# First stage of a streaming-encoder block: another order of column sums, transposes, modulation and masks, and another estimate of transfers in the planner

## The chip, the cores and the metric

The kernel runs on one core of one Trainium2 chip. The metric is the device time of one execution in microseconds (us). Engines are TensorE (PE; its weight loads are listed apart as PEld), VectorE (DVE), ScalarE (ACT), GpSimd (POOL) and SyncE (SP), whose queue starts nearly all transfers. TensorE's clock is shown as the share of full speed that was granted.

## The reference, cut to what matters

One layer of a post-norm encoder block on x of 256 rows by 1024, with a conditioning vector c:

```python
mod = silu(c) @ w_ada + b_ada            # six rows of 1024: sh1, sc1, g1, sh2, sc2, g2
u   = LN(x) * (1 + sc1) + sh1
x   = LN_1(alpha * x + (1 + g1) * Mixer(u))
u   = LN(x) * (1 + sc2) + sh2
x   = LN_2(alpha * x + (1 + g2) * MoE(u))
```

The mixer projects u by one matrix `w_in` of 1024 by 6680. Its first 1536 columns are q, k and v of eight attention heads; the others feed gated linear attention and the gates. The MoE sends each row to 4 of 32 experts. All data are float32.

## The kernel before

**Stages.** The first stage makes q, k and v (columns 0 to 1535 of `w_in`), together with the modulation that u needs. Then come the other projections, attention and the gated linear attention, the branch projections, the output projection, the router, and at last the 32 experts one after the other, whose weights (12 MB each) stream through a ring of buffers. The schedule is written out by hand: each engine executes its instructions in the order in which the program issues them, and waits where one isn't ready.

**The first stage.** The contraction over 1024 is cut into eight steps of 128. For step k two loads are queued on SP, in the order a0, w0, a1, w1 and so on: `first["a", k]` holds 256 columns of `w_ada` (128 of sh1 and 128 of sc1, for all 1024 rows, 1.05 MB in two transfers, rows of 128 elements), `first["w", k]` holds 128 rows of `w_in` by 1536 columns (0.79 MB, rows of 512 elements). `done(...)` hands a buffer back to the ring, which queues the next load. Small loads (`small_loads`) are queued behind step 0.

In each step:

- `ada_sum(k)`: sixteen products of TensorE (listed so; eight in the program) that sum silu(c) times `w_ada` into a bank of PSUM, in four strips of partitions.
- `ada_cols(k, ...)`: VectorE copies the sums to SBUF (`mod`, 128 by 256), TensorE multiplies the copy by a column of `stack` (four listed products), which adds the strips and turns the row into columns; VectorE adds the bias into `shc` (scale and shift as two columns), ScalarE makes `uh` (u rounded to the short float32 format of the matrix products) from the transposed normalized x (`nT`), VectorE makes u in full and `ul = u - uh`.
- `row_parts(k)`: ScalarE rounds the `w_in` rows to `wh`; the rest `wl = w - wh` is made by VectorE (first 512 columns) and GpSimd (second 512 columns), and for v by GpSimd alone. For k = 0 GpSimd makes both halves.
- `three(...)`: each product of u and w is done in three, `wh uh`, `wh ul`, `wl uh`. For q and k these are 24 products of 128x256 in a step, accumulated in four banks (`pqk`), for v six of 128x512 (`pv`).
- two calls of `next(ms)`: the next pieces of the generator `masks`, which builds constants on VectorE that later stages use. Its first piece has thirteen operations, the others three or none.

Ahead of the steps, x (two blocks of 128 rows, `xn[0]`, `xn[1]`) is normalized, block 0 by ScalarE and block 1 by VectorE, and `x_T(hf, tb)` turns half `hf` of block `tb` (four transposes by TensorE, copied out of PSUM by ScalarE for block 0 and by VectorE for block 1).

The order before is: normalize both blocks; transposes of half 0; column sum 0; `row_parts(0)`; modulation 0; transposes of half 1; then for each k: column sum k+1, all 24 products of q and k, `row_parts(k+1)`, modulation k+1, the products of v, two mask pieces.

**The planner.** Behind the first stage, the main products are laced with side tasks (attention scores, gates, row sums). When a side task's next part is issued is decided while the program is built, by `Pace`, a clock per engine and one for the transfers (`at["DMA"]`), advanced by estimated costs. `Pace.dma` estimates a load's end; `lag` is the time from one engine's result to another's use, 1.0 where the earlier access is a transfer.

Of the kernel before, what the change touches and what calls it, by code (L numbers as in the profile page):

```python
# [11 lines left out]
F32R = mybir.dt.float32r  # L12
BF16 = mybir.dt.bfloat16
I32 = mybir.dt.int32
AF = mybir.ActivationFunctionType
OP = mybir.AluOpType
# [4 lines left out]
KC = D // 128  # L21
# [17 lines left out]
FLAT = "p a b -> p (a b)"  # L39
# [40 lines left out]
class Pace:  # L80
# [108 lines left out]
    def dma(self, out, src, size):  # L189
        start = self.at.get("DMA", 0.0)  # L190
        ks = self.blocks(out) if out.space != bass.MemoryType.DRAM else []
        for k in ks:
            w, t = self.last.get(k, ("DMA", 0.0))
            start = max(start, t + self.lag(w, "DMA"))
        end = self.at["DMA"] = start + size / (270000.0 if src.ap[-1][1] <= 128 else 350000.0 if src.ap[-1][1] <= 512 else 400000.0)
        self.note("DMA", [], ks, end)


# [179 lines left out]
def block_kernel(ctx, tc, x, c, w_ada, b_ada, w_in, fox_f_bias, w_gla_gate, b_gla_gate, gla_norm_g,  # L378
# [4 lines left out]
    PE, DVE, ACT, POOL, SP = [Eng(e, n, pace) for e, n in (  # L383
        (nc.tensor, "PE"), (nc.vector, "DVE"), (nc.scalar, "ACT"), (nc.gpsimd, "POOL"), (nc.sync, "SP"))]
# [43 lines left out]
    ring = Ring(new, both, mate, SP)  # L428
# [5 lines left out]
    mm, aux = Bufs(*bank[0:4]), Bufs(*bank[4:8])  # L434
# [4 lines left out]
    gle = Bufs(*cut("GL", 1024))  # L439
# [22 lines left out]
    xn = []  # L462
# [5 lines left out]
    first = {}  # L468
# [139 lines left out]
    def mean_var(st):  # L608
        mv = per.tile([128, 4], F32, tag="mv", bufs=6, name="mv")
        DVE.bn_aggr(mv[:, 0:2], st.rearrange(FLAT))  # L610
        return mv

    def rstd(mv):
        ACT.activation(mv[:, 3:4], mv[:, 1:2], AF.Ln, bias=eps_t)
        ACT.activation(mv[:, 2:3], mv[:, 3:4], AF.Exp, scale=-0.5)

    nT = gst.now([128, 4, T]), gst.now([128, 4, T])
    for tb in range(2):
        st = bn_tile()
        for i in range(2):  # L620
            DVE.bn_stats(st[:, i, :], xn[tb][:, i * 512:(i + 1) * 512])
        mv = mean_var(st)
        rstd(mv)
        if tb:
            DVE.tensor_scalar(xn[tb], xn[tb], mv[:, 0:1], mv[:, 2:3], op0=OP.subtract, op1=OP.mult)
        else:
            DVE.scalar_tensor_tensor(mv[:, 3:4], mv[:, 0:1], -1.0, mv[:, 2:3], op0=OP.mult, op1=OP.mult)
            ACT.activation(xn[tb], xn[tb], AF.Identity, bias=mv[:, 3:4], scale=mv[:, 2:3])


    strict = small("strict", [128, 128], BF16)
# [8 lines left out]
    def masks():  # L640
        trio = consts.now([128, 128])
        DVE.tensor_scalar(trio, jp, 0.0, None, op0=OP.is_ge)
        DVE.tensor_scalar(strict, jp, 0.0, None, op0=OP.is_gt)
        DVE.tensor_scalar(after, jp, 0.0, NEG, op0=OP.is_gt, op1=OP.mult)
        DVE.tensor_copy(identb, ident)
        DVE.memset(onesb, 1.0)
        DVE.tensor_copy(trior[:, 0:128], trio)
        DVE.tensor_copy(trior[:, 128:256], ones)
        xr = consts.now([128, 128], I32)
        DVE.tensor_tensor(xr, pi, ji, op=OP.bitwise_xor)  # L650
        xrf = consts.now([128, 128])
        DVE.tensor_copy(xrf, xr)
        DVE.tensor_scalar(tri64, xrf, 64.0, 1.0 / 16.0, op0=OP.is_lt, op1=OP.mult)
        DVE.tensor_tensor(tri64, tri64, trio, op=OP.mult)
        upm = consts.now([128, 128])
        DVE.scalar_tensor_tensor(upm, jp, 0.0, xrf, op0=OP.is_gt, op1=OP.mult)
        a = consts.now([128, 64])
        yield
        for L in LEVELS:
            yield  # L660
            m = lvl[L] = small(f"lv{L}", [128, 64])
            u3 = upm.rearrange("p (n two l) -> p n two l", two=2, l=L)[:, :, 1, :]
            DVE.tensor_scalar(m.rearrange("p (n l) -> p n l", l=L), u3, float(L), None, op0=OP.is_ge)
            DVE.tensor_scalar(a.rearrange("p (n l) -> p n l", l=L), u3, float(2 * L), None, op0=OP.is_lt)
            DVE.tensor_tensor(m, m, a, op=OP.mult)
# [8 lines left out]
    def split(src, *engines):  # L674

        t, n = pair.now(), src.free_size()
        wh, wl = t[:, 0:n].bitcast(F32R), t[:, 1024:1024 + n].bitcast(F32R)
        ACT.activation(wh, src, AF.Copy)
        if not engines:
            either(wl, src, wh, OP.subtract, WLBIAS)  # L680
        for i, e in enumerate(engines):
            c = slice(i * 512, (i + 1) * 512)
            e.tensor_tensor(wl[:, c], src[:, c], wh[:, c], op=OP.subtract)
        return wh, wl, t
# [60 lines left out]
    def done(i):  # L745
        ring.done(i)
        if last_first in ring.got:
            ring.recall(*early, "YB1")

    def x_T(hf, tb):  # L750
        p = aux.now()
        for q in range(4):
            k = hf * 4 + q
            PE.transpose(p[:, q * 128:(q + 1) * 128], xn[tb][:, k * 128:(k + 1) * 128], ident)
        d, s = nT[hf][:, :, tb * 128:(tb + 1) * 128], p.rearrange("p (a b) -> p a b", a=4)
        if tb:
            DVE.tensor_copy(d, s)
        else:
            ACT.activation(d, s, AF.Copy)
        aux.put(p)  # L760

    def ada_sum(c):

        w = ring[first["a", c]].rearrange("p k a n -> p k (a n)")
        s = pa[:, c % 2 * 256:c % 2 * 256 + 256]
        for k in range(KC):
            j = k % 4
            PE.matmul(s[32 * j:32 * j + 32, :], csrep[:, k, :], w[:, k, :],
                      start=(k < 4), stop=(k >= 4), skip_group_check=True)
        done(first["a", c])  # L770
        return s

    def ada_cols(c, s):
        mod = la.now([128, 256])
        DVE.tensor_copy(mod, s)
        for i in range(2):
            PE.matmul(pb[:, 2 * c + i:2 * c + i + 1], mod[:, i * 128:(i + 1) * 128], stack[:, 0:1], start=True, stop=True)
        la.put(mod)
        DVE.tensor_tensor(shc[:, :, c], pb[:, 2 * c:2 * c + 2], cols[:, 16 + c:32:8], op=OP.add)
        u = nT[c // 4][:, c % 4, :]  # L780
        ACT.activation(uh[:, c, :], u, AF.Identity, bias=shc[:, 0, c:c + 1], scale=shc[:, 1, c:c + 1])
        DVE.tensor_scalar(u, u, shc[:, 1, c:c + 1], shc[:, 0, c:c + 1], op0=OP.mult, op1=OP.add)
        DVE.tensor_tensor(ul[:, c, :], u, uh[:, c, :], op=OP.subtract)

    def row_parts(k):
        w = ring[first["w", k]]
        qk = split(w[:, 0:2, :].rearrange(FLAT), DVE if k else POOL, POOL)
        v = split(w[:, 2, :], POOL)
        done(first["w", k])
        return qk, v  # L790
# [3 lines left out]
            if reg[n] in pair.free:  # L794
                pair.free.remove(reg[n])

    LA = 2
    ms = masks()
    for tb in range(2):
        x_T(0, tb)  # L800
    pa, pb = aux.now(), aux.now()
    sums = {0: ada_sum(0)}
    ahead = {0: row_parts(0)}
    ada_cols(0, sums.pop(0))
    for tb in range(2):
        x_T(1, tb)
    gle.put(*xn)
    pqk, pv = [mm.now() for _ in range(4)], [aux.now(), aux.now()]
    for k in range(KC):
        qk, v = ahead.pop(k)  # L810
        if k + 1 < KC:
            sums[k + 1] = ada_sum(k + 1)
        for cb in range(8):
            cs = slice(cb * 128, (cb + 1) * 128)
            three(pqk[cb // 2][:, (cb % 2) * T:(cb % 2 + 1) * T], (qk[0][:, cs], qk[1][:, cs]), u_of(k),
                  k == 0 and cb % 2 == 0, k == KC - 1)
        pair.put(qk[2])
        if k + 1 < KC:
            ahead[k + 1] = row_parts(k + 1)
            ada_cols(k + 1, sums.pop(k + 1))  # L820
        if k == KC - 1:
            back()
            for q in range(LA):
                prep(q)
            pf = ff_mm()
            fb.put(hold["wfg"])
        for tb in range(2):
            t = slice(tb * 128, (tb + 1) * 128)
            three(pv[tb], (uh[:, k, t], ul[:, k, t]), v[:2], k == 0, k == KC - 1)
        pair.put(v[2])  # L830
        if k == KC - 2:
            aux.put(pa, pb)
        next(ms, None)
        next(ms, None)
        if k == 0:
            small_loads()
        if k == 6:
            for _ in ms:
                pass
            wfg = hold["wfg"]  # L840
            own("YA")
            both("YA")
            pair.free.append(reg["W2"])
            wfh, wfl = hold["wf"] = [shaped(t, [128, KC, 32], F32R) for t in cut("YA", 256, 0, 2)]
            ACT.activation(wfh, wfg, AF.Copy)
            DVE.tensor_tensor(wfl, wfg, wfh, op=OP.subtract)
# [1280 lines left out]
```

## Time and profile before

| | us |
|---|---|
| median of 3 runs | 1266.03 |
| lowest and highest run | 1264.9, 1266.1 |
| profiled execution | 1263.44 |
| its span, first to last instruction | 1261.7 |

| engine | busy us | share of span | instructions |
|---|---|---|---|
| PE | 1167.8 | 93% | 6482 |
| DVE | 492.5 | 39% | 1070 |
| ACT | 266.4 | 21% | 526 |
| POOL | 71.2 | 6% | 52 |

The mean granted clock of TensorE was 0.991, and 471.57 MB were moved, 374 GB/s over the span. Times in the profile count from the start of the span. Names are those of buffers: regions that share memory have joined names (`LQFA`, `YB1NB`), `U1U` holds `uh` and `ul`, `W` and `ADAM` hold `wh` and `wl`, `GL` holds x, `GSGX` holds `nT`, `YAW` the constants of the masks. Nearly every instruction is issued through one helper, so all show its line, L209. Matmuls are pipelined and their ends are modelled: starts are the surer reading. Spans on POOL are rough.

### The profile page before, as it was taken

The page shows a single profiled execution, that of the slowest core. Times are in us where ns is not written, and L with a number is a line of the kernel's source. Part 1 is how long each engine was busy: PE and PEld are TensorE (multiplying, and loading weights), DVE is VectorE, ACT ScalarE, POOL GpSimd, SP SyncE. Part 2 cuts the span into 40 slices and gives each one's busy share as a digit, 9 for nine tenths or more (in the row PEclk, how much of TensorE's full clock was granted, in tenths as well). Part 3 has the DMA queues.
Part 4 walks back from the last instruction along what each step waited for, and adds up shares of the span by engine and source line. Part 5 has one row for each costly group of instructions (what it writes and reads, how often), then busy time and mean ns, then how long its engine had stood idle before and what let it go on. Part 6 is the DMA issues. An engine that isn't in the chain of part 4 may idle for free. (4 is left out here: it accounts for less than half of the span.)

```text
span 1261.7 us, 15755 instructions
## 1 busy us (share of the span) xinstructions
PE 1167.8 (93%) x6482; PEld 598.8 (47%) x6482; DVE 492.5 (39%) x1070; ACT 266.4 (21%) x526; POOL 71.2 (6%) x52
## 2 busy tenths in 40 slices
PE   6999999999899999999998989898989898898995
PEld 4887778898443434344342424343433333342432
DVE  5546654487443323333223222223333232223233
ACT  4345445444411101011010101010111101010101
POOL 3412322010000000000000000000000000000000
PEclk9999999999899999999999999999999999999998
DMA  9953347995999999999999999999999999999994
GB/s 306 314 185 115 135 166 278 397 352 211 394 428 426 429 426 429 426 429 425 430 426 428 427 428 428 428 428 427 428 427 429 427 427 429 426 430 426 430 408 144
DMA packets 74118, 471.57 MB, mean 374 GB/s; under 512 B 8637, under 2 KB 29149, under 8 KB 47034
## 3 DMA queue, kind: packets, MB, share of 16 engines
q1 hardware_dynamic: 73850, 470.23, 91.3%
q8 instruction: 53, 0.87, 0.3%
q10 hardware_dynamic: 192, 0.27, 0.1%
q14 instruction: 23, 0.19, 0.0%
HBM read 469.44 MB, written 1.05 MB: 373 GB/s over the span
## 5 line engine op out<-in xcount | busy, mean ns | idle before, releaser
L209 PE MATMUL b<-U1U,W 128*128 128x256 f32 (+1 forms) x840 | 143.0, 410 | 11.3 <-DMA U1U<-in_w_down_dram 8.4
L209 DVE COPY W<-b 128x512 f32<-128x512 f32 x32 | 22.1, 692 | 295.3 <-PE b L209 295.3
L209 PEld LDWEIGHTS b<-U1U,W 128*128 128x128 f32 (+1 forms) x840 | 86.7, 169 | 69.7 <-issue 61.3
L209 DVE TENSOR_TENSOR W<-b,SP 128x512 f32<-128x512 f32 (+1 forms) x33 | 22.3, 676 | 218.4 <-PE b L209 218.4
L209 DVE TENSOR_TENSOR GL<-b,GL 128x512 f32<-128x512 f32 x124 | 77.0, 683 | 54.0 <-PE b L209 54.0
L209 PE MATMUL b<-YB1NB,W 128*64 128x512 f32 (+2 forms) x440 | 89.4, 528 | 4.5 <-DVE SP L209 3.9
L209 PE MATMUL b<-R2YB,W 128*64 128x512 f32 x344 | 78.3, 595 | 9.8 <-DMA R2YB<-in_w_down_dram 7.9
L209 PE MATMUL b<-YAW,W 128*64 128x512 f32 (+1 forms) x384 | 82.2, 554 | 4.0 <-DVE SP L209 4.0
L209 PE MATMUL b<-GSGX,W 128*64 128x512 f32 x336 | 76.2, 595 | 10.1 <-DMA GSGX<-in_w_down_dram 8.2
L209 PE MATMUL b<-R0R,W 128*64 128x512 f32 (+1 forms) x368 | 80.2, 578 | 5.3 <-DMA R0R<-in_w_up_dram 4.9
L209 PE MATMUL b<-GVKB,W 128*64 128x512 f32 x336 | 78.1, 608 | 6.1 <-DMA GVKB<-in_w_up_dram 6.1
L209 ACT ACTIVATE W<-b 128x512 f32<-128x512 f32 x32 | 19.1, 598 | 302.0 <-PE b L209 302.0
L209 PE MATMUL b<-LQFA,W 128*64 128x512 f32 x336 | 78.1, 607 | 5.0 <-DMA LQFA<-in_w_up_dram 5.0
L209 PE MATMUL b<-ADAM,W 128*64 128x512 f32 x336 | 75.9, 593 | 4.3 <-DVE SP L209 2.7
L209 ACT ACTIVATE SP<-b 128x256 f32<-128x256 f32 (+1 forms) x34 | 12.8, 377 | 306.1 <-PE b L209 306.1
L209 PEld LDWEIGHTS b<-W,QA 128*128 128x128 f32 x512 | 63.1, 200 | 14.1 <-DVE GL L209 11.4
L209 PE MATMUL b<-W,QA 128*128 128x128 f32 x512 | 66.4, 289 | 1.4 <-DVE W L209 1.4
L209 PE MATMUL b<-W,SP 64*128 64x512 f32 (+1 forms) x264 | 63.9, 602 | 0.5 <-DVE W L209 0.5
L209 PEld LDWEIGHTS b<-YB1NB,W 128*64 128x64 f32 (+1 forms) x440 | 35.7, 146 | 55.1 <-issue 45.2
L209 ACT ACTIVATE W<-b,scol 128x128 f32<-128x128 f32 x124 | 47.0, 457 | 65.7 <-PE b L209 59.9
L209 POOL TENSOR_TENSOR GL<-GL,QB 128x512 f32<-128x512 f32 x2 | 2.9, 1426 | 981.5 <-ACT GL L209 981.4
L209 PEld LDWEIGHTS b<-YAW,W 128*64 128x64 f32 (+1 forms) x384 | 30.6, 144 | 52.5 <-issue 45.0
(335 smaller groups left out, 1374.7 us busy)
## 6 DMA issues: line engine op xcount, KB each, us to landing
GVKB<-in_w_up_dram SPq DMA_DIRECT2D x21, 2048.0 KB
R0R<-in_w_up_dram SPq DMA_DIRECT2D x20, 2048.0 KB
LQFA<-in_w_up_dram SPq DMA_DIRECT2D x20, 2048.0 KB
YB1NB<-in_w_up_dram SPq DMA_DIRECT2D x11, 2048.0 KB
U1U<-in_w_up_dram SPq DMA_DIRECT2D x11, 2048.0 KB
YAW<-in_w_up_dram SPq DMA_DIRECT2D x11, 2048.0 KB
GSGX<-in_w_up_dram SPq DMA_DIRECT2D x11, 2048.0 KB
YAW<-in_w_down_dram SPq DMA_DIRECT2D x10, 2048.0 KB
```

Source lines behind the costliest of these rows:

```text
L209: r = f(*a, **k)
```

## The change

In the first stage:

- Both blocks of x are normalized by VectorE, after the statistics of both.
- Column sum 0 is issued ahead of the transposes. `ada_sum` now also issues VectorE's copy of the sums, so that the copy stands directly behind the sum in VectorE's order.
- For k = 0 the split of w is written out: ScalarE rounds, GpSimd makes the second half of `wl`, and VectorE the first half, behind modulation 0. Column sum 1 and the transposes of half 1, block 0, follow; those of block 1 stand in the middle of the products of step 0.
- In each step the 24 products of q and k are cut in two runs of 12. `row_parts(k+1)` and modulation k+1 are issued between the two runs (modulation first for k = 0) instead of behind them.
- `masks` yields after every one to three operations: twelve pieces instead of eight.

In the planner, `Pace.dma` no longer adds a lag between two transfers into one buffer, and takes 310 in place of 270 GB/s for rows of up to 128 elements.

```diff
-            start = max(start, t + self.lag(w, "DMA"))
-        end = self.at["DMA"] = start + size / (270000.0 if src.ap[-1][1] <= 128 else 350000.0 if src.ap[-1][1] <= 512 else 400000.0)
+            start = max(start, t + (self.lag(w, "DMA") if w != "DMA" else 0.0))
+        end = self.at["DMA"] = start + size / (310000.0 if src.ap[-1][1] <= 128 else 350000.0 if src.ap[-1][1] <= 512 else 400000.0)
...
+    mvs = []
     for tb in range(2):
         st = bn_tile()
         for i in range(2):
             DVE.bn_stats(st[:, i, :], xn[tb][:, i * 512:(i + 1) * 512])
-        mv = mean_var(st)
-        rstd(mv)
-        if tb:
-            DVE.tensor_scalar(xn[tb], xn[tb], mv[:, 0:1], mv[:, 2:3], op0=OP.subtract, op1=OP.mult)
-        else:
-            DVE.scalar_tensor_tensor(mv[:, 3:4], mv[:, 0:1], -1.0, mv[:, 2:3], op0=OP.mult, op1=OP.mult)
-            ACT.activation(xn[tb], xn[tb], AF.Identity, bias=mv[:, 3:4], scale=mv[:, 2:3])
+        mvs.append(mean_var(st))
+        rstd(mvs[tb])
+    for tb, mv in enumerate(mvs):
+        DVE.tensor_scalar(xn[tb], xn[tb], mv[:, 0:1], mv[:, 2:3], op0=OP.subtract, op1=OP.mult)
...
         DVE.tensor_scalar(strict, jp, 0.0, None, op0=OP.is_gt)
+        yield
         DVE.tensor_scalar(after, jp, 0.0, NEG, op0=OP.is_gt, op1=OP.mult)
         DVE.tensor_copy(identb, ident)
+        yield
         DVE.memset(onesb, 1.0)
...
         done(first["a", c])
-        return s
-
-    def ada_cols(c, s):
         mod = la.now([128, 256])
         DVE.tensor_copy(mod, s)
+        return mod
+
+    def ada_cols(c, mod):
...
-        qk = split(w[:, 0:2, :].rearrange(FLAT), DVE if k else POOL, POOL)
+        qk = split(w[:, 0:2, :].rearrange(FLAT), DVE, POOL)
...
     LA = 2
     ms = masks()
-    for tb in range(2):
-        x_T(0, tb)
     pa, pb = aux.now(), aux.now()
-    sums = {0: ada_sum(0)}
-    ahead = {0: row_parts(0)}
-    ada_cols(0, sums.pop(0))
-    for tb in range(2):
-        x_T(1, tb)
-    gle.put(*xn)
-    pqk, pv = [mm.now() for _ in range(4)], [aux.now(), aux.now()]
+    mods = {0: ada_sum(0)}
+    for tb in range(2):
+        x_T(0, tb)
+    ahead = {}
+    src = ring[first["w", 0]][:, 0:2, :].rearrange(FLAT)
+    t0 = pair.now()
+    wh0, wl0 = t0[:, 0:1024].bitcast(F32R), t0[:, 1024:2048].bitcast(F32R)
+    ACT.activation(wh0, src, AF.Copy)
+    POOL.tensor_tensor(wl0[:, 512:1024], src[:, 512:1024], wh0[:, 512:1024], op=OP.subtract)
+    ada_cols(0, mods.pop(0))
+    DVE.tensor_tensor(wl0[:, 0:512], src[:, 0:512], wh0[:, 0:512], op=OP.subtract)
+    v = split(ring[first["w", 0]][:, 2, :], POOL)
+    done(first["w", 0])
+    ahead[0] = (wh0, wl0, t0), v
+    mods[1] = ada_sum(1)
+    x_T(1, 0)
+    pqk = [mm.now() for _ in range(4)]
     for k in range(KC):
         qk, v = ahead.pop(k)
-        if k + 1 < KC:
-            sums[k + 1] = ada_sum(k + 1)
-        for cb in range(8):
+        if 0 < k < KC - 1:
+            mods[k + 1] = ada_sum(k + 1)
+        qk_mm(k, qk, range(4))
+        if k == 0:
+            x_T(1, 1)
+            gle.put(*xn)
+            pv = [aux.now(), aux.now()]
+        if k + 1 < KC:
+            if k:
+                ahead[k + 1] = row_parts(k + 1)
+            ada_cols(k + 1, mods.pop(k + 1))
+            if not k:
+                ahead[k + 1] = row_parts(k + 1)
+        qk_mm(k, qk, range(4, 8))
         pair.put(qk[2])
-        if k + 1 < KC:
-            ahead[k + 1] = row_parts(k + 1)
-            ada_cols(k + 1, sums.pop(k + 1))
```

`qk_mm(k, qk, cbs)` issues the products of q and k for the column blocks `cbs`, three for each, as the loop over `cb` did.

## Rows read from the trace of the kernel before

**Rows 1.** Windows by stage: busy time of each engine, granted clock, transfer share, GB/s.
```profile
67.50:318.00 250.50, 248.67 (x1782) 202.49 (x1780) 153.95 (x247) 122.18 (x207) 43.59 (x24) 1.00 0.63 227
318.00:1262.00 944.00, 864.25 (x4261) 352.56 (x4261) 301.61 (x732) 118.64 (x282) 2.85 (x2) 0.99 0.99 417
310.00:320.00 10.00, 7.87 (x59) 6.03 (x57) 8.05 (x19) 5.30 (x16) 0.00 (x0) 1.00 0.30 92
```
**Rows 2.** Windows in the first stage, columns as in group 1.
```profile
0.00:5.50 5.50, 0.26 (x1) 0.18 (x1) 1.68 (x6) 1.59 (x2) 1.00 (x8) 1.00 0.59 190
5.50:9.50 4.00, 0.02 (x1) 0.00 (x0) 3.28 (x9) 1.62 (x3) 0.00 (x0) 1.00 1.17 318
11.50:15.00 3.50, 2.96 (x22) 1.29 (x21) 1.11 (x2) 1.58 (x2) 2.08 (x2) 1.00 1.20 317
16.50:49.50 33.00, 30.97 (x266) 24.34 (x258) 22.77 (x59) 12.53 (x18) 14.51 (x13) 1.00 1.12 331
```
**Rows 3.** Timeline of TensorE, first stage: start, time, what [idle before, releaser].
```profile
11.26 1.12 PE L209 MATMUL b<-ident,GL 128*128 128x128 f32 x4 [0.47 <-DVE GL L209]
12.31 1.94 PE L209 MATMUL b<-YB1NB,LQFA 128*32 128x256 f32 x16
...
15.25 1.07 PE L209 MATMUL b<-ident,GL 128*128 128x128 f32 x8
16.25 1.07 PE L209 MATMUL b<-QB,LQFA 128*32 128x256 f32 x16
17.25 3.14 PE L209 MATMUL b<-U1U,W 128*128 128x256 f32 x24
...
23.16 3.13 PE L209 MATMUL b<-U1U,ADAM 128*128 128x256 f32 x24
27.73 0.61 PE L209 MATMUL b<-stack,LQFA 128*128 128x1 f32 x4 [1.44 <-DVE LQFA L209]
...
30.78 3.13 PE L209 MATMUL b<-U1U,W 128*128 128x256 f32 x24
33.75 0.50 PE L209 MATMUL b<-stack,LQFA 128*128 128x1 f32 x4
...
36.68 3.13 PE L209 MATMUL b<-U1U,ADAM 128*128 128x256 f32 x24
...
43.20 3.13 PE L209 MATMUL b<-U1U,W 128*128 128x256 f32 x24
...
55.49 3.13 PE L209 MATMUL b<-U1U,W 128*128 128x256 f32 x24
...
60.77 1.46 PE L209 MATMUL b<-U1U,ADAM 128*128 128x256 f32 x10 [0.19 <-DVE U1U L209]
```
**Rows 4.** Timeline of VectorE, steps 1 and 2: masks, subtraction, copy, ul.
```profile
24.13 1.32 DVE L209 TENSOR_TENSOR tri<-tri,YAW 128x128 f32<-128x128 f32 x1
25.37 1.37 DVE L209 SCALAR_TENSOR_TENSOR YAW<-YAW 128x128 f32<-128x128 int32 x1
26.66 0.68 DVE L209 TENSOR_TENSOR W<-GVKB,W 128x512 fp32r<-128x512 f32 x1
27.27 0.41 DVE L209 COPY LQFA<-b 128x256 f32<-128x256 f32 x1
...
29.65 0.43 DVE L209 TENSOR_TENSOR U1U<-GSGX,U1U 128x256 fp32r<-128x256 f32 x1
```
**Rows 5.** Timeline of GpSimd, the same steps.
```profile
24.01 2.58 POOL L209 TENSOR_TENSOR W<-GVKB,W 128x512 fp32r<-128x512 f32 x2 [2.48 <-ACT W L209]
```
**Rows 6.** The tile shc's readers, all eight steps: lowest, median, highest ns.
```profile
L209 ACT ACTIVATE U1U<-GSGX,shc x8: 600/602/602, 15.7 to 59.2; 128x256 fp32r<-128x256 f32 x8
L209 DVE TENSOR_SCALAR GSGX<-GSGX,shc x8: 411/414/476, 16.3 to 59.8; 128x256 f32<-128x256 f32 x8
```
**Rows 7.** Timeline of ScalarE, start of the first stage.
```profile
10.83 0.60 ACT L209 ACTIVATE GSGX<-b 128x512 f32<-128x512 f32 x1 [0.47 <-PE b L209]
11.78 1.58 ACT L209 ACTIVATE W<-QA 128x1024 fp32r<-128x1024 f32 x2 [0.35 <-DMA QA<-in_w_in_dram]
```

More of the change, by code (lines that the diff above doesn't have):

```diff
@@ L648, in masks @@
         DVE.tensor_copy(trior[:, 128:256], ones)
+        yield
         xr = consts.now([128, 128], I32)
@@ L652, in masks @@
         DVE.tensor_copy(xrf, xr)
+        yield
         DVE.tensor_scalar(tri64, xrf, 64.0, 1.0 / 16.0, op0=OP.is_lt, op1=OP.mult)
         DVE.tensor_tensor(tri64, tri64, trio, op=OP.mult)
+        yield
         upm = consts.now([128, 128])
@@ L657, in masks @@
         a = consts.now([128, 64])
-        yield
         for L in LEVELS:
@@ L795, in back, with qk_mm @@
                 pair.free.remove(reg[n])
-    LA = 2
-    ms = masks()
-    for tb in range(2):
-        x_T(0, tb)
-    pa, pb = aux.now(), aux.now()
-    sums = {0: ada_sum(0)}
-    ahead = {0: row_parts(0)}
-    ada_cols(0, sums.pop(0))
-    for tb in range(2):
-        x_T(1, tb)
-    gle.put(*xn)
-    pqk, pv = [mm.now() for _ in range(4)], [aux.now(), aux.now()]
-    for k in range(KC):
-        qk, v = ahead.pop(k)
-        if k + 1 < KC:
-            sums[k + 1] = ada_sum(k + 1)
-        for cb in range(8):
+    def qk_mm(k, qk, cbs):
+        for cb in cbs:
             cs = slice(cb * 128, (cb + 1) * 128)
@@ L816, in block_kernel @@
                   k == 0 and cb % 2 == 0, k == KC - 1)
+    LA = 2
+    ms = masks()
+    pa, pb = aux.now(), aux.now()
+    mods = {0: ada_sum(0)}
[15 more added lines that the diff above has]
+    pqk = [mm.now() for _ in range(4)]
+    for k in range(KC):
+        qk, v = ahead.pop(k)
+        if 0 < k < KC - 1:
[12 more added lines that the diff above has]
+        qk_mm(k, qk, range(4, 8))
         pair.put(qk[2])
-        if k + 1 < KC:
-            ahead[k + 1] = row_parts(k + 1)
-            ada_cols(k + 1, sums.pop(k + 1))
         if k == KC - 1:
```

## The prediction

> **What bounds the kernel now.** I read the windows by stage first, because the share of busy time over the whole span mixes stages. The expert stage, from 318 us on, moves 417 GB/s with the transfer engines busy 0.99 of the time, while just ahead of it, from 310 to 320 us, they are busy 0.30; between 67.5 and 318 us TensorE is busy 248.67 of 250.5 us and the transfers are at 0.63 [rows 1]. So the last stage is a stream of fixed length that starts when the stages before it free their buffers, and those stages are bound by TensorE. A microsecond that the first stage gives up should come off the end one for one.
>
> Then the transfers of the first stage, in windows: x (1.05 MB) is in at about 5.5 us (190 GB/s), and from 16.5 to 49.5 us the rate is 331 GB/s [rows 2]. A step k of the eight brings 1.05 MB of `w_ada` and 0.79 MB of `w_in`, 1.84 MB, so the transfers need 1.84 / 0.331 = 5.5 us a step.
>
> Then TensorE's timeline of that stage [rows 3]. The q and k products of the steps begin at 17.25, 23.16, 30.78, 36.68, 43.20, (one not shown), 55.49 us, and the last step's at 60.77. The step from 30.78 to 36.68 has no wait in it: 5.90 us, just above the transfers' 5.5. The others show the waits by difference. 23.16 to 30.78 is 7.62, 1.72 too long; 36.68 to 43.20 is 6.52, 0.62 too long; 43.20 to 55.49 is two steps in 12.29, 0.49 too long. The seventh carries no column sum, whose price is the 1.00 us between 16.25 and 17.25, so the last step would begin at 55.49 + 5.90 - 1.00 = 60.39; its first product runs alone, the rest from 60.77, which counts as a start at 60.77 - 0.13 = 60.64 (a product is 3.13 / 24 us), 0.25 late. The waits sum to 1.72 + 0.62 + 0.49 + 0.25 = 3.08 us. That is all that a better order can take from the steps.
>
> The reason stands on VectorE. The small products against `stack` (27.73 us) wait 1.44 us for the copy of the modulation sums, and that copy stands behind mask instructions, two of which take 1.32 and 1.37 us, and a subtraction of 0.68 [rows 3, 4]. The two slow ones lie inside GpSimd's two subtractions (24.01 us, 2.58 in all) [rows 5].
>
> **The change part by part.** *Steps 1 to 7.* The copy of the sums now stands directly behind the column sum, ahead of the subtraction; the `stack` products stand in the middle of the q and k products instead of behind them; the masks come in twelve pieces, two a step. No product is added or dropped, so the step stays at 5.90. Is the copy in time? Count from the start of uh(k+1) on ScalarE (0.60 us); u and ul follow on VectorE (0.41 and 0.43), done at +1.5 [rows 4, 6]. ScalarE's casts let GpSimd work from about +1.7 to +4.3 (two of 1.29), and masks that fall into that time end at +4.3 to +4.7. The next column sum is over at about +3.7, the copy (0.41) at up to +5.1. The `stack` products of the next step are due 5.90 us after those of this one, at about +5.2, since uh starts some 0.7 behind them. So the copy just fits: the 3.08 go, and 0 to 0.6 us of new waits may come (five steps with masks, 0.1 each); I take 0.1. The chain behind it (uh, u, ul) is then over about 2 us ahead of the products that need it, which covers the last step's 0.25 too.
>
> *Step 0, the start.* The column sum of step 0 moves ahead of the transposes and meets its transfer. 1.05 MB behind x at 318 GB/s is in at 8.8 us [rows 2]; with the lag that `w_in` shows (all bytes at about 11.3, ScalarE let go at 11.78 [rows 7]) I take 9.5. The sixteen took 1.94 us at 12.31 and 1.07 at 16.25, at the same granted clock of 1.00 [rows 2, 3]; I take 1.94, so it ends at 11.45. Both normalizations on VectorE are over by 11.2 even in the old order (transposes of the second block at 11.26), so they are hidden behind it, the one that moves off ScalarE included. Four transposes, 1.12, to 12.6; ScalarE's copy 0.60, to 13.2 [rows 3, 7]. Behind it in ScalarE's order stands the cast wh0 (two thirds of 1.58, 1.05), to 14.3, and only then uh(0). The other branch, four more transposes (13.7), `stack` products 0.6 and an add of 0.16, is ready at 14.5. So uh(0) is done at 15.1, and u, ul and the half of wl0 that moves from GpSimd to VectorE (0.41, 0.43, 0.68) end at 16.7 if nothing blocks them. TensorE itself is free at 16.6: the second column sum's data is in at 15.0 (1.05 MB from 11.5 at 317 GB/s is 14.8), 1.0 for it, 0.54 for four transposes at the price of the eight at 15.25.
>
> GpSimd, however, works on wl0's other half from 14.35 to 15.65 and, once ScalarE has cast v, on v's part from 15.7 to 17.0. Every mask operation of rows 4 that came up during a GpSimd subtraction ended when that ended. Blocked so, u ends at 15.9, ul at 17.3, wl0 at 18.0, and the products effectively start two products earlier, at 17.75. Between 16.6 and 17.75 us, then; before it was 17.25. Four transposes (0.54) now fall inside step 0, so step 1 starts 5.91 + 0.54 later: at 23.05 to 24.2, against 23.16. Nearest to the blocked case by rows 4, I take 23.9: 0.75 us lost, bounds -0.1 and +1.05.
>
> The Trainium skill, SBUF — State Buffer, section Who interferes with whom, says that a VectorE operation with two SBUF inputs, or in a two-port mode, and a GpSimd operation shut each other out for the whole instruction, the first to issue winning. The trace agrees (1.32 us for a 128x128 operation beside a GpSimd one of 1.29), and by that rule alone the start loses the full 1.05 and the mask wait below the full 1.0, which makes the whole gain 0.9; without it the gain is 3.2.
>
> *Step 1 once more.* In step 0 uh(1) comes ahead of the casts, and GpSimd's two subtractions for step 1 run late. With S for step 0's start: transposes at S+1.5, the copy of their result and the add to S+3.1, uh to S+3.7, the cast of w to S+4.8, VectorE's half of wl1 to S+5.5 and GpSimd's two from there to S+8.1. Two mask pieces (four operations) come up at S+5.5. Blocked by both, they end at S+8.4, the copy at S+8.9; the `stack` products of step 1 are due at S+6.45 plus half of the q and k products (33.75 - 30.78 = 2.97, half is 1.5), S+7.95 [rows 3]. The wait is 0 to 1.0; I take 0.5, because VectorE may slip small operations in before GpSimd has the port.
>
> *Transfers and queues.* The order on SP's queue stays: each load is still freed by the same column sum or cast and in the same order, the small loads behind step 0. The last step's weights are in at 5.5 + 8 × 5.5 + 0.5 = 50 us, and its products start near 59, so the transfers stay hidden; their slack is what covers the earlier casts.
>
> *The corrected estimate.* It moves no data. The planner's clock for transfers was 1.94 + 1.0 + 1.94 + 2.25 = 7.1 us a step by its own formula and becomes 5.6, less than its TensorE cost; it decides where side tasks are issued behind 67.5 us. TensorE idles only 1.83 us there [rows 1], so a better order gives at most 1.8; a worse one has no such bound. I take 0 and keep ±1.
>
> Sum: 3.08 - 0.75 - 0.5 - 0.1 = 1.7 us. Bounds from the first stage: 3.08 + 0.1 = 3.2 and 3.08 - 1.05 - 1.0 - 0.6 = 0.4. The profiled execution took 1263.44 us (its span 1261.7, with 1.7 around it), 2.6 under the median of the runs, 1266.03. So the changed kernel would take 1261.7 in such an execution, and 1264.3 beside the median.
>
> **Rivals.** *No collisions.* VectorE's operations come up just ahead of GpSimd's instead of behind them; step 1 starts at 23.05 and nothing waits: gain 3.2, 1262.8 us. Against it stand the blocked operations of rows 4.
>
> *Given back behind the stage.* The transfers of the next stage follow the same saturated queue and come no sooner, so its first products wait for them: gain 0, 1266.0. Against it: TensorE's order puts 5 us of other products between, and transfers are at 0.63 from 67.5 us on [rows 1].
>
> *Slower, by the planner.* Between 67.5 and 318 us side tasks are issued at other places, and their small products stand in TensorE's order ahead of VectorE's results. The 1.44 us at 27.73 is what one such misplacement costs. From the third on the gain is lost, three at 1.44 being 4.3, 2.6 more than 1.7: 1268.6. For it: the step estimate changes by 1.5 us. Against: behind the first stage the estimate, like the trace, is bound by TensorE, so most places should stay.
>
> **How the numbers follow.** Forecast 0.56, no collisions 0.22, given back 0.10, planner 0.12. What a measurement of this kernel can tell from no change is about 0.2%, 2.5 us. Faster by more: no collisions, and 0.08 of the forecast where the planner adds its part, 0.30. Within: 0.48 + 0.10 = 0.58. Slower: 0.12. The range reaches from 1262.0 (no collisions and a little from the planner) to 1267.0 (all collisions and the planner's 1 us against), and leaves out most of the slower case. The forecast's own range is 1262.8 to 1265.6.
>
> **What would show it.** Right: step starts 5.9 apart from the second on, no wait of the `stack` products above 0.3 us but in step 1, step 1 at 23.5 to 24.2, the last step at 58.5 to 59.5, TensorE's idle time from there to 318 as before. Wrong: step 0 at 16.6 (no collisions), mask operations that push the copy past the `stack` products in each step, or idle time of TensorE behind 67 us that is over 3 us.

## The result and the profile after

The changed kernel took 1275.12 us, median of 4 runs (1273.52 to 1277.1), against 1265.55 for the kernel before in the same comparison: 1.0078 of it, 95% interval 1.0066 to 1.009. It is 0.8% slower, and the forecast of 1264.3 was 10.8 us too low. The profiled execution took 1275.1 us, its span is 1273.3, 11.6 more than before (by the medians the loss is 9.6).

TensorE's timeline of the first stage in the changed kernel, columns as in [rows 3]:

```profile
10.05 1.93 PE L209 MATMUL b<-YB1NB,LQFA 128*32 128x256 f32 x16 [4.32 <-DMA YB1NB<-in_w_ada_dram]
...
15.58 1.94 PE L209 MATMUL b<-QB,LQFA 128*32 128x256 f32 x16 [1.05 <-DMA QB<-in_w_ada_dram]
...
18.22 2.91 PE L209 MATMUL b<-U1U,W 128*128 128x256 f32 x12
...
26.10 1.70 PE L209 MATMUL b<-U1U,ADAM 128*128 128x256 f32 x12
29.23 0.60 PE L209 MATMUL b<-stack,LQFA 128*128 128x1 f32 x4 [1.43 <-DVE LQFA L209]
...
33.69 1.70 PE L209 MATMUL b<-U1U,W 128*128 128x256 f32 x12
...
57.29 1.70 PE L209 MATMUL b<-U1U,W 128*128 128x256 f32 x12
...
62.10 2.08 PE L209 MATMUL b<-U1U,ADAM 128*128 128x256 f32 x16
```

From 33.69 on the steps follow 5.90 us apart (57.29 - 33.69 is four steps in 23.60) with no wait: that part of the forecast holds. The start gives it back: step 0 at 18.22 against 17.25, step 1 at 26.10 against 23.16, and one wait of 1.43 us left. The last step begins at 62.10 against 60.64, 1.46 late instead of 1.7 early. Part of that is this execution's pace: twelve products take 2.91 us at 18.22 and 1.70 at 26.10. The windows print a granted clock of 1.00 there, but that is what they print where the trace has no entry of the clock, and its first entry is at 21.7 us (14.1 in the kernel before). Four transposes take 0.97 us at 20.93, just ahead of it, and four 0.60 at 126.55.

VectorE in step 0 and in the steps' first masks, which answers to [rows 4]:

```profile
16.15 1.43 DVE L209 TENSOR_TENSOR U1U<-GSGX,U1U 128x256 fp32r<-128x256 f32 x1
...
24.93 1.31 DVE L209 TENSOR_SCALAR YAW<-YAW 128x128 f32<-128x128 int32 x1
26.16 1.41 DVE L209 TENSOR_SCALAR strict<-YAW 128x128 bf16<-128x128 int32 x1
27.41 0.23 DVE L209 TENSOR_SCALAR after<-YAW 128x128 bf16<-128x128 int32 x1
27.56 1.28 DVE L209 CAST identb<-ident 128x128 bf16<-128x128 f32 x1
28.76 0.41 DVE L209 COPY LQFA<-b 128x256 f32<-128x256 f32 x1
```

and GpSimd beside it, which answers to [rows 5]:

```profile
14.70 2.61 POOL L209 TENSOR_TENSOR W<-QA,W 128x512 fp32r<-128x512 f32 x2 [13.05 <-ACT W L209]
24.36 3.04 POOL L209 TENSOR_TENSOR ADAM<-GVKB,ADAM 128x512 fp32r<-128x512 f32 x2 [7.06 <-ACT ADAM L209]
...
27.45 2.54 POOL L209 TENSOR_TENSOR W<-GVKB,W 128x512 fp32r<-128x512 f32 x2
```

Three of the four mask operations take 1.28 to 1.41 us beside GpSimd's subtractions, and the copy that the `stack` products wait for stands behind them: the wait of 27.73 in [rows 3] is back in the same step. (The first mask piece of the kernel before has twelve operations, not thirteen.)

The first stage ends 1.35 us late, of 11.6. The rest lies behind. TensorE between 76 and 335 us in the changed kernel:

```profile
76.17 0.88 PE L209 MATMUL b<-U1U,YAW 128*128 128x256 f32 x6
79.25 0.83 PE L209 MATMUL b<-ident,ADAM 128*128 128x128 f32 x4 [2.20 <-DMA ADAM<-in_b_up_dram]
79.73 3.89 PE L209 MATMUL b<-U1U,YAW 128*128 128x256 f32 x18
...
132.59 0.61 PE L209 MATMUL b<-YB1NB 8*128 8x384 f32 x2 [2.84 <-ACT GVKB L209]
...
334.43 0.18 PE L209 MATMUL b<-msk,strict 128*128 128x32 bf16 x1 [1.02 <-DVE msk L209]
```

The product on `msk`, in the router, stands at 323.76 in the kernel before:

```profile
67.74 0.87 PE L209 MATMUL b<-U1U,W 128*128 128x256 f32 x6
...
323.76 0.18 PE L209 MATMUL b<-msk,strict 128*128 128x32 bf16 x1 [1.03 <-DVE msk L209]
```

The changed kernel begins the products of 67.74 at 69.09, 1.35 late. So of 11.6 us, 1.35 come from the first stage, 9.3 from the work between (265.3 us against 256.0), and 0.9 from the experts. Windows of the changed kernel, columns as in [rows 1]:

```profile
67.50:318.00 250.50, 245.11 (x1733) 199.48 (x1731) 153.46 (x230) 118.89 (x197) 50.29 (x25) 0.98 0.62 224
...
79.80:83.20 3.40, 3.40 (x18) 3.40 (x17) 0.69 (x1) 0.00 (x0) 0.00 (x0) 0.51 0.80 175
103.50:106.90 3.40, 3.40 (x18) 2.30 (x17) 1.31 (x6) 1.88 (x11) 0.00 (x0) 0.52 0.85 265
134.20:137.40 3.20, 3.20 (x15) 1.14 (x17) 3.16 (x5) 0.91 (x2) 3.20 (x3) 0.52 0.02 5
318.00:330.00 12.00, 9.86 (x62) 7.88 (x62) 7.58 (x18) 5.76 (x16) 0.00 (x0) 1.00 0.39 135
```

Two things make up the 9.3: two new waits, 2.20 us for the load of `b_up` at 79.25 and 2.84 us for ScalarE at 132.59 (5.0 together), and three stretches in which TensorE is busy throughout at a granted clock of 0.51 to 0.52, the level of 1.2 GHz, where before it was granted 1.00 all the way from 67.5 to 318 us. Each lasts 3.4 us (the third runs on to 137.7), and 3.4 us at half the pace cost 1.7, three times 5.1. That is 10.1 for 9.3 us; counted between the same two products, TensorE's idle time grew by 4.9 us and its busy time by 4.4. The expert stage's stream starts later by what came before it: from 318 to 330 us the transfers are at 135 GB/s, where the kernel before moves 412 in the same window.

### The profile page after: what moved, and what is told of

Its sections match the earlier page's. It is cut to its first block, busy times and chain, and to the rows that moved or that the text cites. A ratio compares the mean times of both kernels' runs of the same rounds, so it can differ in the third digit from the quotient of the medians.

```text
span 1273.3 us, 15759 instructions
## 1 busy us (share of the span) xinstructions
PE 1172.7 (92%) x6482; PEld 604.7 (47%) x6482; DVE 501.7 (39%) x1070; ACT 267.2 (21%) x525; POOL 75.5 (6%) x52
## 3 DMA queue, kind: packets, MB, share of 16 engines
HBM read 469.44 MB, written 1.05 MB: 369 GB/s over the span
## 5 line engine op out<-in xcount | busy, mean ns | idle before, releaser
L209 PE MATMUL b<-U1U,W 128*128 128x256 f32 (+1 forms) x840 | 146.0, 413 | 11.2 <-DMA U1U<-in_w_down_dram 8.4
L209 PEld LDWEIGHTS b<-W,QA 128*128 128x128 f32 x512 | 63.1, 200 | 14.1 <-DVE GL L209 11.4
```

Of the source, the lines that this page charges most:

```text
L209: r = f(*a, **k)
```

## The experiments

**Which half of the change it is.** The changed kernel with the old estimate, and the kernel before with the new one. The first, `new_order_old_estimate`, takes both lines of `Pace.dma` back:

```diff
-            start = max(start, t + (self.lag(w, "DMA") if w != "DMA" else 0.0))
+            start = max(start, t + self.lag(w, "DMA"))
-        end = ... (310000.0 if src.ap[-1][1] <= 128 ...
+        end = ... (270000.0 if src.ap[-1][1] <= 128 ...
```

> The changed first stage with the planner's estimate of transfers as it was before. Behind the first stage the program then issues side tasks at the same places as the kernel before. Theory A (the estimate moves side tasks to bad places, which costs about 8 us): the first stage is as in the changed kernel, last step's products near 62.1 us, 1.35 us late at the first product behind it (68.87 against 67.52), and the middle stage is as before, so 1266.9 us. Rival B (the first stage's order itself costs the 10 us, the middle only follows): about 1275.

Measured: 1265.37 us, 1.0005 (0.9995 to 1.0016). The second, `old_order_new_estimate`, makes these two edits alone in the kernel before:

> The first stage as before with the corrected estimate. Theory A: first product behind the first stage at 67.5 us as before, then the waits that the changed kernel shows (TensorE for b_up near 77, for ScalarE near 130, three stretches at the lower clock), 1275.1 - 1.35 = 1273.8 us. Rival B: 1265.5.

Measured: 1278.93 us, 1.011 (1.0096 to 1.0125). Its waits between 62 and 330 us are the two of the changed kernel:

```profile
PE b L209 <- ACT GVKB L209: 2.8, 1, 2.8
PE b L209 <- DMA ADAM<-in_b_up_dram: 2.2, 1, 2.2
```

So the loss comes with the estimate, which moves no data. The first stage alone is worth nothing that can be measured. That the second run is slower even than the changed kernel has its mark in the clock: in its profile the granted clock is 0.50 for 3.4 us from 28.6 and from 79.8 us, and for 6.8 us from 103.7 and from 134.4.

**What the estimate changes.** This much follows from the program without a run. Of the two edits in `Pace.dma` only the dropped lag alters an instruction: with the lag kept and 310 GB/s, the program is that of before, and it is too if the lag is kept for loads under 0.1 MB alone. Those are twelve loads into one buffer: eight rows of `b_ada` and four quarters of `b_up`. The lag had put them one behind another, so that the planner took `b_up` to be there 17.1 us after its clock of TensorE stood when it queued them; without it, 6.9 us. One side task takes its due time straight from them, the transposes of `b_up`:

```python
        yield pace.when(bup)
        p = yield from aux.get()
        for q in range(4):
            PE.transpose(p[:, q * 128:(q + 1) * 128], hidden(bup, q), ident)
```

A task that isn't due holds one of the few places of the run list, the tasks in progress. When this one falls due earlier, the next tasks start earlier, and every later side task moves, as does the choice between VectorE and GpSimd that the planner makes for some operations by its clocks. The following runs move only that due time, or only its consequences.

`bias_loaded_early`: the changed kernel, every side task kept where it stands (the kernel reads the changed kernel's choices from a recorded string of bits instead of the planner's clocks), but `b_up` loaded among the small loads of step 0 into a buffer that is free then.

```diff
+        bup = hold["bup"] = gle.now()
+        for i in range(4):
+            SP.dma_start(bup[32 * i:32 * i + E, 0:512], b_up[0][:, i * 512:(i + 1) * 512])
...
-        for i in range(4):
-            SP.dma_start(bup[32 * i:32 * i + E], b_up[0][:, i * 512:(i + 1) * 512])
```

> The changed kernel with every side task issued where the changed kernel issues it, but b_up loaded with the small loads of step 0 into a buffer of its own, so that its transposes find it. Theory S (the wait for b_up and the lower clock behind it are part of the loss, the rest comes from the places of the other side tasks): the wait of 2.2 us near 77 and the 3.4 us at half clock behind it (1.7 us) go, the wait of 2.8 us near 130 stays: 1275.1 - 3.9 = 1271.2. Rival C (the rest is only a consequence of that first wait): 1265 to 1267. Rival N (the wait was covered): 1275.

Measured: 1272.11 us, 1.0041 (1.0028 to 1.0054). The wait for the load is gone, and with it the low stretch at 80 us; the other wait stays, at 127.59, 2.84 us, with a low stretch behind it. So the late load costs 3.0 us by the medians (4.7 by the ratios), and half of the loss or more has another cause. The low stretch of 103.5 us is missing too, although the products ahead of it stand as they did, so some of the gain may be the execution's. The runs spread from 1267.66 to 1273.11.

`due_earlier_by_8`: the kernel before, with the old estimate, and the due time 8 us earlier.

```diff
-        yield pace.when(bup)
+        yield pace.when(bup) - 8.0
```

> The kernel before with its old estimate and one number changed: the task of the bias transposes is due 8 us earlier. By the planner's clocks it was due 17.1 us ahead of TensorE, now 9.1, while the corrected estimate made it 6.9. If the due time of this one task is what the corrected estimate changes, the loss comes back without the correction: a time of 1270 to 1279. Rival (the estimate works through other loads): 1265.7.

Measured: 1274.39 us, 1.006 (1.0045 to 1.0075), although nothing waits for `b_up` (the transposes start at 81.04). The row that is left in its waits:

```profile
PE b L209 <- ACT GVKB L209: 2.8, 1, 2.8
```

Places alone can cost this much. The profile also has two low stretches, of 3.4 us from 102.1 and of 6.8 us from 129.4. `due_later_by_4` is the best start of the first stage (below) with the corrected estimate and `+ 4.0` in that line:

> The best kernel so far (start as before, new steps, no masks in step 0; 1262.4 us) with the corrected estimate, and the task of the bias transposes due 4 us later than the estimate has b_up landed. A third order of side tasks. Theory S (the places of side tasks decide, whether b_up is waited for or not): no wait for b_up, yet 1265 to 1275, with waits and lower clock where VectorE and GpSimd meet. Rival C (only the issue ahead of the data hurts): 1262.4.

Measured: 1261.81 us, 0.9964 (0.9951 to 0.9977). The first theory, 1265 to 1275 us with waits in any third order of the side tasks, did not come true: this order has no new wait. The time is near the rival's 1262.4, but the rival's reason, that only an issue ahead of the data hurts, does not fit `due_earlier_by_8`, which loses 8.6 us by the medians (1274.39 against 1265.77) without one. Some orders cost and others do not, whether `b_up` is waited for or not. And `changed_due_later_by_4` is the changed kernel itself with that one number:

> The changed kernel with one number altered: the due time of the bias transposes is 4 us later; first stage, corrected estimate and all else as in the changed kernel, and the side tasks stand at the places of due_later_by_4. If the due time of that one task is all that the correction spoils, the time is that of new_order_old_estimate, 1265.4 us (1264 to 1267), no wait for b_up and none of 2.8 us near 130 us. If the new first stage is itself at odds with a corrected estimate, or the loss is spread over all places, 1270 to 1275 us.

Measured: 1264.82 us, 0.9992 (0.9983 to 1.0001). The window that was 245.11 us busy at 0.98:

```profile
67.50:318.00 250.50, 250.15 (x1795) 204.49 (x1793) 153.61 (x245) 121.75 (x204) 44.09 (x24) 1.00 0.64 229
```

The wait for `b_up` and the one near 130 us are both gone. One number in one task's due time takes back all of the loss (1275.12 to 1264.82), with the corrected estimate in place. That rules out that a corrected estimate or the new first stage is bad in itself.

**Why the places cost a wait at 132.59.** In the changed kernel that product writes a bank which ScalarE has to empty first. ScalarE, columns as before:

```profile
129.56 1.06 ACT L209 ACTIVATE GL<-GL 128x1024 f32<-128x1024 f32 x1 [1.78 <-DVE GL L209]
130.52 1.04 ACT L209 ACTIVATE YAW<-R0R 128x1024 fp32r<-128x1024 f32 x1
131.47 1.06 ACT L209 ACTIVATE GVKB<-b 128x512 f32<-128x512 f32 x2
```

It empties the bank at 131.47, behind an exponential that waited 1.78 us for VectorE's `GL`. VectorE made it here:

```profile
120.05 3.04 DVE L209 TENSOR_TENSOR GL<-GVKB 128x512 f32<-128x512 f32 x2
...
124.61 2.56 DVE L209 TENSOR_TENSOR W<-R0R,W 128x1024 fp32r<-128x1024 f32 x1 [1.19 <-ACT W L209]
127.09 2.38 DVE L209 TENSOR_TENSOR GL<-GVKB 128x512 f32<-128x512 f32 x2
```

beside GpSimd's

```profile
120.19 2.35 POOL L209 TENSOR_TENSOR GL<-GVKB 128x1024 f32<-128x1024 f32 x1
123.70 2.38 POOL L209 TENSOR_TENSOR GSGX<-QB,GL 128x1024 f32<-128x1024 f32 x1 [1.17 <-ACT GL L209]
126.05 2.27 POOL L209 TENSOR_TENSOR LQFA<-QB,GL 128x512 f32<-128x512 f32 x1
```

`levels_on_vector` is `bias_loaded_early` with the three GpSimd operations of this last group given to VectorE, at the same places (lines of the helper are L218 in these two kernels). The edit sets three bits of the recorded string, from which this line chooses the engine:

```diff
-    "...7cfe6c80232c15c834755b01...
+    "...7cfe6c802b2c15c934f55b01...
...
         (DVE if placed() else POOL).tensor_tensor(o, a, b, op=op)
```

> bias_loaded_early with three operations of the level and decay tasks ahead of 130 us (GL and GSGX of 1024 columns, LQFA of 512) on VectorE instead of GpSimd, at the same places. If it is GpSimd and VectorE running beside each other that delays ScalarE's evacuation and so the products near 130 us, the wait of 2.8 us shrinks to 1.5 us or less and the time falls below 1272.1 us, to 1268 to 1270.5 us. If VectorE only gets longer by what GpSimd loses, the wait and the time stay, 1271 to 1274 us.

Measured: 1266.86 us, 1.0011 (0.9999 to 1.0023), 5.2 us under `bias_loaded_early` by the medians and 3.8 by the ratios. VectorE has three operations more and is sooner done. The two `GL` subtractions that took 3.04 us (at 120.05 above) take 2.47 with a third, of 1024 columns, among them; the 2.56 and 2.38 us behind them (124.61, 127.09) become 1.23 and 1.29:

```profile
115.55 2.47 DVE L218 TENSOR_TENSOR GL<-GVKB 128x1024 f32<-128x1024 f32 x3
...
119.02 1.23 DVE L218 TENSOR_TENSOR W<-R0R,W 128x1024 fp32r<-128x1024 f32 x1 [0.67 <-ACT W L218]
...
121.41 1.29 DVE L218 TENSOR_TENSOR GL<-GVKB 128x512 f32<-128x512 f32 x2
```

and TensorE's wait falls from 2.84 to

```profile
126.18 0.62 PE L218 MATMUL b<-YB1NB 8*128 8x384 f32 x2 [0.95 <-ACT GVKB L218]
```

with the granted clock at 1.00 over all of 67.5 to 318 us:

```profile
67.50:318.00 250.50, 248.71 (x1777) 203.58 (x1775) 155.28 (x241) 121.65 (x204) 43.65 (x22) 1.00 0.64 228
```

Four loads placed elsewhere and three operations on another engine undo the loss but for 0.1%. That is a second way to the same time, and it names the place: GpSimd beside VectorE. Two things change there, and the run doesn't part them. The operations end sooner when nothing runs beside them, and GpSimd itself is slower at the moved ones: 2.38 us for `GSGX` of 1024 columns, where VectorE takes 1.21 (130.45 in the changed kernel). In the changed kernel ScalarE waits 0.98 us for GpSimd's `GL` at 122.57, ahead of the chain that ends at the bank.

**The first stage by itself.** `old_start_new_steps` has the start of before (normalization, transposes, column sum 0, step 0's split) with the new steps, the twelve mask pieces and the old estimate.

> The start as before (transposes ahead of the column sum, one normalization on ScalarE, both halves of wl0 on GpSimd), the steps in the new order, masks in twelve pieces, old estimate. Theory A with a slow start by TensorE's lower clock: step 0 starts at 17.25 as before, the waits of steps 3, 4 and 7 (0.62, 0.49, 0.25) go, step 1's stays between 0.5 and 1.4 because its masks still meet GpSimd: 1263.3 to 1264.5 us. Rival: the new order in the steps costs something itself, 1265.5 or more.

Measured: 1263.81 us, 0.9991 (0.9982 to 1.0). Step 1 stands at 23.26, and its `stack` products still wait 1.18 us. `old_start_masks_later` also takes the masks out of step 0:

```diff
-        next(ms, None)
-        next(ms, None)
+        if k:
+            next(ms, None)
+            next(ms, None)
```

> As the run before, but no masks in step 0, so that two pieces a step fall to steps 1 to 6. If masks beside GpSimd are what makes step 1's stack products wait, all 3.0 us of waits go: 1262.5 us, steps 5.9 apart from the first. Rival: something else (the copy behind VectorE's subtraction) makes them wait: the same time as the run before.

Measured: 1262.44 us, 0.9977 (0.9968 to 0.9987). Its TensorE:

```profile
17.43 1.70 PE L209 MATMUL b<-U1U,W 128*128 128x256 f32 x12
...
23.33 1.70 PE L209 MATMUL b<-U1U,ADAM 128*128 128x256 f32 x12
24.87 0.50 PE L209 MATMUL b<-stack,LQFA 128*128 128x1 f32 x4
...
29.23 1.70 PE L209 MATMUL b<-U1U,W 128*128 128x256 f32 x12
...
57.64 3.03 PE L209 MATMUL b<-U1U,ADAM 128*128 128x256 f32 x24
```

All steps are 5.90 apart from the first on, and the last begins at 57.64, 3.0 us earlier than before: the whole 3.08 of the waits. The profiled span is 3.0 us shorter, and the median 3.3 under that of before in the same comparison (1265.74; by the interval 1.6 to 4.1), so a microsecond here does come off the end one for one, as far as the runs can tell. In the new order with the old estimate, by contrast, the start costs what the steps give:

```profile
18.32 1.46 PE L209 MATMUL b<-U1U,W 128*128 128x256 f32 x10 [0.22 <-DVE W L209]
...
24.42 1.70 PE L209 MATMUL b<-U1U,ADAM 128*128 128x256 f32 x12
27.54 0.61 PE L209 MATMUL b<-stack,LQFA 128*128 128x1 f32 x4 [1.43 <-DVE LQFA L209]
...
60.41 3.03 PE L209 MATMUL b<-U1U,ADAM 128*128 128x256 f32 x24
```

`warm_start` adds 23 products of `ident` by itself ahead of the first transposes of `old_start_masks_later`, so that TensorE is at its upper level sooner:

> The best kernel so far with 23 dummy products of a 128x128 constant on TensorE while it idles ahead of the first transposes (9 ahead of the small transpose, 14 behind it). If the lower clock of the start is on the path (sixteen products of the first column sum in 1.94 against 1.07 us, transposes in 1.12 against 0.54), step 0 starts about 1.2 us earlier, near 16.2: 1261.2 us. Rival (transfers and the chain over ScalarE and VectorE bound the start): 1262.4.

Measured: 1261.37 us, 0.9958 (0.9945 to 0.997). The time named, 1261.2, came, but not by the way named: the interval overlaps that of the kernel without them, and step 0 began at 18.97 in its profile, not near 16.2 and later than 17.43. The added products ran at 0.23 us each up to 5.6 us and at 0.12 behind it, and from 12.4 us the granted clock was 0.50 for 6.8 us. Whether these products help is not settled.

The best version with nothing left out or added is `due_later_by_4`: the steps of the change, the start of before, no masks in step 0, the corrected estimate, and one due time 4 us later; 0.9964 of before, some 13 to 14 us under the changed kernel. Whether the estimate helps in it is not shown: without it (`old_start_masks_later`) the interval reaches 0.9968 to 0.9987.

## Why the prediction was wrong

- **"The corrected estimate ... I take 0 and keep ±1"** is the step that failed. It cost 9.3 us in the profile between 69 and 334 us, and 10 to 13 us by the runs (1265.37 to 1275.12 with the new order, 1265.7 to 1278.93 with the old). The working looked at the step estimate, 7.1 against 5.6 us, and argued that the planner is bound by TensorE, so that most places stay. But `lag` applies to every pair of loads into one buffer, and the twelve small ones behind the stage are those by which it alters the program. Each could have been counted: the twelve loads stand in the program, and `pace.when(bup)` is the due time taken straight from them. In the term's place the runs show two waits, 5.0 us together, and low stretches of the clock, 5.1.
- **The rival "Slower, by the planner"** was the true case, at 0.12, and too small: three misplacements of 1.44 us, 1268.6. Two waits came, of 2.20 and 2.84 us, and each was followed by a stretch at half the clock that cost 1.7 more, with a third stretch at 103.5 us besides. Its mechanism was half right: the first is a product issued ahead of its data, the second is a chain over VectorE and GpSimd, side by side.
- **The range** kept ±1 for a cost that the text itself said has no bound on the slow side; 1267.0 as its upper end did not follow from that sentence.
- **Steps 2 to 7** at 5.90 us without waits: right, in every run with the new steps. The 3.08 us are there, and `old_start_masks_later` shows them at the end of the kernel too.
- **Step 0, the start**: -0.75 was forecast, with bounds to -1.05; it is -1.26 in the execution with the old estimate (24.42 against 23.16) and -2.94 in the changed kernel's (26.10). GpSimd blocked VectorE as forecast: `ul` took 1.43 us beside the subtractions at 14.70 and ended at 17.58, forecast 17.3. Missed were the transfers, taken to be ready for the column sums at 9.5 and 15.0 and in fact at 10.05 and 15.58, and TensorE's pace: in the changed kernel's profile twelve products take 2.91 us at 18.22, where 1.70 is their later time. The working read 1.94 against 1.07 us for the column sums as a difference at one granted clock, 1.00; the trace has no entry of the clock at 12.31. When the later pace comes differs by execution, so the 1.7 us between the two profiles of the same first stage are no effect of the order.
- **Step 1's wait**: 0.5 was taken between 0 and 1.0; it is 1.43 in both profiles. The mask operations were blocked as in the worse case (1.28 to 1.41 us for three of the four), and without masks in step 0 the wait is gone. The sentence on the Trainium skill, SBUF — State Buffer, section Who interferes with whom, by which VectorE and GpSimd shut each other out for a whole instruction and the gain would be 0.9, came nearer than the value taken; the first stage gave 0.2 (60.41 against 60.64).
- **One for one**: right, as far as the runs can tell. What the first stage or the middle gains or loses comes off or on at the end, since the stream of the experts only starts then.

What stays open: why TensorE's clock fell near 103 us, where no wait stands ahead, but four microseconds of small products, some of them with 8 rows to an operand. All twelve profiles have that run of products, and the clock fell behind it in four: the changed kernel, `old_order_new_estimate`, `due_earlier_by_8`, and `old_start_new_steps` (0.50 from 95.9 to 99.3 us), which takes 1263.81 us all the same. So that stretch isn't shown to belong to the places, and 1.7 of the 9.3 us may be the execution's. That the half-clock stretches at 80 and 134 us follow from the waits ahead of them is read from their places; in `bias_loaded_early` and `levels_on_vector` the stretch went with its wait, which agrees.

## What to carry to other kernels

When an order of instructions is made from estimated costs, an edit of an estimate is a change of the whole order behind it: list which due times move, and price that as an unknown with a slow side of its own, not as nothing. A term that is more exact for large loads can make a plan worse where the old error was a margin that something lived on; test the margin alone, by adding a constant to the one due time. And before a waiting product is blamed on what it waits for, look at which two engines ran beside each other one link earlier: moving three operations to the busier engine gave back 4 to 5 us. Before an execution's loss is booked to an order, look for low stretches of the clock that other executions lack.

## What the runs showed of the hardware

Small loads are slow for their size. SP's queue in the changed kernel:

```profile
73.55 2.31 SPq L209 DMA_DIRECT2D ADAM<-in_b_ada_dram  x8
75.90 1.70 SPq L209 DMA_DIRECT2D ADAM<-in_b_up_dram  x4
```

The eight rows of `b_ada` are 2 KB each and the four of `b_up` 64 KB; the queue alone spends 0.29 and 0.43 us on each, and the product that waits for the last starts at 79.25, 1.65 us after the queue is through. The Trainium skill, DMA: Bandwidth & Descriptors, section on the anatomy of one DMA, states for GpSimd's path a fixed cost of about 2 us for each transfer, whatever its size; from SP's queue this trace shows about as much, 2.05 us from the start of the last issue (77.2) to the product. The planner's formula prices a load by its bytes alone, and the lag of 1.0 us for each had stood in for that. How much of the 2.20 us at 79.25 is due to it is not shown: the twelve loads also stood behind GpSimd's memset of the buffer for the rows of `b_ada` (72.57 to 73.52), for which the queue had waited 3.8 us.

A wait of TensorE can cost nearly twice itself. Behind the waits of 2.20 and 2.84 us the granted clock fell to 0.50, 0.5 and 1.7 us after the engine had resumed and although it was busy again, and stayed there for 3.4 us. Between 62 and 140 us the twelve profiles have six waits of 2.2 to 2.84 us, and a low stretch of 3.4 or 6.8 us goes with each; in two of them it begins while the engine still waits. Behind the wait of 1.43 us at 29.23 the clock stayed at 1.00 in the changed kernel's profile, and in that of `changed_due_later_by_4` it fell behind the same wait (0.58 from 29 to 33 us); of the nine profiles with a wait of 1.2 to 1.5 us in that step, it fell in four. A wait's price read off the waits alone is too low by what follows.

Two engines can be slower than one. Two subtractions of 128x512 took VectorE 3.04 us beside GpSimd's 2.35 and 1.29 alone; with three operations moved from GpSimd to VectorE, VectorE's group was done sooner too.
